# Order of side work in a two-layer decoder trunk: FFN sums leave PSUM behind the next split, modulation sums are planned away from the heads, two turned blocks are kept, the rope's swap moves to VectorE

## The chip, the cores and the metric

The kernel runs on one core of one Trainium2 chip. Its time is device microseconds of one execution; the version before was run three times, and the median stands for it. Five engines of the core take part: TensorE (PE in the profile; PEld are its weight loads), VectorE (DVE), ScalarE (ACT), GpSimd (POOL) and the queue of SyncE (SP), from which nearly all loads are issued.

## The reference, cut to what matters

One sequence of 256 tokens with 2048 features passes two layers. Layer 0 mixes by causal pooling, layer 1 by latent attention with 16 heads; each is followed by a SwiGLU feed-forward net (FFN) of width 5632. Every part reads `modulate(rmsnorm(x))`, with shift and scale out of a vector `c`, and adds its output times a gate that comes from `c` as well:

```python
shift_m, scale_m, gate_m, shift_f, scale_f, gate_f = jnp.split(sc @ mod_w[i] + mod_b[i], N_MOD, axis=-1)
ckv = rmsnorm(h_kv @ w_dkv, kv_norm)          # 512 wide, shared by all heads
k_nope, v = ckv @ w_uk, ckv @ w_uv            # per head 128 and 128
k_rope = apply_rope(h_kv @ w_kr, cos, sin)    # 64 wide, one for all heads
cq = rmsnorm(h @ w_dq, q_norm)
q = cq @ w_uq                                 # per head 128 + 64, rope on the 64
o = softmax(causal(q k)) v;  y = o @ w_o
x = x + gate_m * y;  x = x + gate_f * (silu(h @ w_gate) * (h @ w_up)) @ w_down
```

All is float32.

## The kernel before, in words

**Products.** A weight matrix is loaded in units of 128 x 2048 elements (1 MB). `split` makes two halves of a unit for TensorE: ScalarE rounds it to the upper half (L374), VectorE subtracts that from the unit to get the lower half (L376). Activations are split alike, and a product is three products: upper x upper, upper x lower, lower x upper. A unit then takes 24 matmuls of 128 x 512 (L398), or, in the keys, 48 of 128 x 256 (L1288). The loads have six buffers (`raw`), the halves six (`hl`, so three units), PSUM has eight banks (`ps`), all handed round in the order of the program.

**Modulation sums.** The products of `c` with `mod_w` and `kv_mod_w` are mostly made by VectorE: `Part.unit` loads 1 MB and sums 128 rows of it against `c` (L210, L211). 168 such units lie in a list, `background`, and are worked off beside other work. `plan(left, units)` sets a rate: so many sums until `left` remain, spread evenly over the next `units` splits. `split` calls `tick`, which starts a sum when the rate says so; `hold` stops that for a while, `release` sets a new rate. The constants `FFN0_UNITS`, `MLA_LATE` and their like (L64, L69) are the numbers behind these calls. When the 16 sums of a gate are there, VectorE adds the bias (L300), TensorE turns the column (L292), and DMAs write it to DRAM and spread it over the 128 partitions (`gate_to`).

**Stages.** After a prologue (pooling mixer) and FFN 0 comes a handover: `then_attention` orders ScalarE, VectorE and TensorE by hand. The last product of FFN 0 (L407) is interleaved with the normalization of the finished token tile: POOL takes the root (L472), the tile is scaled by it (`scale`, L476: the first 512 features on VectorE, the second on POOL), turned by TensorE (L482), modulated on ScalarE and VectorE (L490 to L503), and multiplied with `w_dkv` (L407; for the third and fourth 512 features L1197). `key_part` (L1208) makes the rotary key. Then `keys_values` runs for four groups of four heads: a unit of `w_uk` (L1288), a unit of `w_uv` (L398). Between the second and third group the hidden blocks of the queries begin: `hidden_q` scales (L530), turns (L540) and modulates (L558 to L560) 512 features each. Four units of `w_dq` give the query latent, `Latent` normalizes and turns it beside the fourth group. Then come the heads, in pairs: `project_heads` (L1368 to L1370, L1288), `probabilities` (L1383 to L1401), `turned` (L1407), `output` (L1414), and last `w_o` and FFN 1.

**FFN.** `down` sums three chunks of the middle layer in PSUM and then moves them at once: for the first group of chunks ScalarE copies them to `x` (L782), later VectorE adds them (L784).

**Rope.** `rope_start` copies the product out of PSUM by ScalarE, once as it is (L843) and once with halves of 32 rows swapped (L845, four instructions); `rope_end` multiplies by `sin_t` and `cos_t` on VectorE (L849, L850) and adds (L852).

Outside the hand-ordered stages a scheduler orders each engine's instructions by priority when the program is built; on the chip each engine runs them in that order.

Of the kernel before, what the change touches and what calls it, by code (L numbers as in the profile page):

```python
# [17 lines left out]
P = 128  # L18
# [45 lines left out]
FFN0_UNITS, MLA_UNITS, HEAD_UNITS, WO_UNITS, FFN1_UNITS = 95, 4, 16, 8, 60  # L64
# [4 lines left out]
LATE, MLA_LATE, WO_LATE = 3, 5, 3  # L69
# [4 lines left out]
def shape_constants():  # L74
# [6 lines left out]
    con[:, C_SIGN] = np.where(q % ROPE < HALF, -1.0, 1.0)  # L81
# [12 lines left out]
def tile_trunk(ctx: ExitStack, tc: tile.TileContext, a: dict, out: bass.AP):  # L94
# [190 lines left out]
    def gate_to(name, first):  # L285
# [163 lines left out]
    class Handover:  # L449
# [24 lines left out]
        def scale(self, tok, j):  # L474
            self.turned[tok, j] = t2k([P, CH]), ps_t().rearrange("p (k t) -> p k t", k=KL), t2k([P, KL, P])
            (dve if j == 0 else pool).tensor_scalar(out=self.turned[tok, j][0], in0=x[:, tok, j * CH:(j + 1) * CH],  # L476
                                                    scalar1=self.rstd[:, tok:tok + 1], scalar2=None, op0=ALU.mult)
# [236 lines left out]
    def ffn(l, hT, gate_name, begun, then):  # L714
# [22 lines left out]

        def down(i):
# [101 lines left out]
    def rope_start(bank):  # L840

        t_ = t2k([P, 2, T])
        act.activation(t_[:, 0, :], bank, AF.Copy)  # L843
        for r in range(0, P, HALF):
            act.activation(t_[r:r + HALF, 1, :], bank[r ^ HALF:(r ^ HALF) + HALF], AF.Copy)  # L845
        return t_

    def rope_end(t_, dsts):
        dve.tensor_tensor(out=t_[:, 1, :], in0=t_[:, 1, :], in1=sin_t, op=ALU.mult)  # L849
        dve.tensor_tensor(out=t_[:, 0, :], in0=t_[:, 0, :], in1=cos_t, op=ALU.mult)  # L850
# [264 lines left out]
    plan(n_all + MLA_LATE, FFN0_UNITS)  # L1115

    hkv, rstd, ckv = None, None, []
# [4 lines left out]
    def then_attention(old, banks, piece):  # L1122
# [6 lines left out]
        split_upper(w[0])  # L1129
        run(h.old(0))  # L1130
# [6 lines left out]
        split_lower(w[0])  # L1137
# [28 lines left out]
        run(b0[2], a1[2], b1[0], b1[1])  # L1166
# [4 lines left out]
        pieces = [scaled(rstd, j, pool) for j in range(2, ND)]  # L1171
        for j in range(2, ND):
            w_ = w_load_of(dkv(j))
            if j == 2:
                wkr = raw_t([P, KD, ROPE])
                sync.dma_start(wkr, a["w_kr"].rearrange("(k p) n -> p k n", p=P))
# [3 lines left out]
            full = [t2k([P, 2, T]) for _ in range(2)]  # L1180
            columns = [[cols[:, i, j * KL + k:j * KL + k + 1] for i in (C_AKV, C_SKV)] for k in range(KL)]
# [3 lines left out]
            for k, (by, plus) in enumerate(columns):  # L1185
# [13 lines left out]
        wkr_h, wkr_l = hl_t([P, KD, 2, ROPE]), hl_t([P, KD, 2, ROPE])  # L1199
        for i in range(2):  # L1200
            act.activation(wkr_h[:, :, i, :], wkr, AF.Copy)
# [3 lines left out]
        def key_part(n):  # L1205
            w_, i = sums[n]
            for k in range(KD):
                pe.matmul(krb[:, :T], lhsT=w_[:, k].rearrange("p i n -> p (i n)"), rhs=hkv[k // KL][:, i, k % KL, :],  # L1208
# [6 lines left out]
        for ks in (slice(0, KD // 2), slice(KD // 2, KD)):  # L1215
            for i in range(2):
                dve.tensor_tensor(out=wkr_l[:, ks, i, :], in0=wkr[:, ks], in1=wkr_h[:, ks, i, :].bitcast(F32),
                                  op=ALU.subtract)
# [72 lines left out]
    release(n_all, MLA_UNITS)  # L1291
# [13 lines left out]
    def last_of_background():  # L1305
        plan(n_all, 0)
# [9 lines left out]
    rope_end(kr_t, [(slice(0, ROPE), krT[0:ROPE, 0, :]), (slice(ROPE, P), krT[ROPE:P, 1, :])])  # L1316
# [261 lines left out]
```

## Time and profile before

| what | value |
|---|---|
| three runs | 1917.03, 1918.83, 1919.51 us; median 1918.83 |
| profiled execution | 1918.19 us, of which the span 1916.4 us |
| TensorE busy | 1862.8 us of the span |
| VectorE, ScalarE, POOL busy | 1402.7, 850.2, 26.9 us |
| mean granted TensorE clock | 0.987 |
| DMA | 574.98 MB, mean 300 GB/s |

The span runs from the first to the last instruction of the program. The profile gives starts and durations of every instruction, what an engine waited for, and by stretches of time the busy share and the granted clock. In it, FFN 0 reaches to about 889 us, the handover and the latent to 938, keys and query latent to 1010, the heads to 1098, `w_o` to 1186, FFN 1 to the end.

### The profile page before, as it was taken

What the parts mean: (1) busy time and instruction counts of PE and PEld (TensorE: products, weight loads), DVE (VectorE), ACT (ScalarE), POOL (GpSimd) and SP (SyncE); (2) the same over time, 40 slices, a digit from 0 to 9 for tenths busy, and PEclk for the clock granted to TensorE, in tenths of its full rate; (3) what the DMA queues carried; (4) which work ended last, traced back from release to release, by engine and by line L of the source; (5) the groups of instructions that cost most, each with busy time, mean ns of one, the idle gap of its engine ahead of it and who ended that gap; (6) DMA issues with size and microseconds to landing.
All of it is one profiled execution on the core that took longest, in us unless ns stands there. A gap on an engine that the chain in (4) does not pass through costs nothing.

```text
span 1916.4 us, 21930 instructions
## 1 busy us (share of the span) xinstructions
PE 1862.8 (97%) x8813; PEld 1507.8 (79%) x8813; DVE 1402.7 (73%) x1391; ACT 850.2 (44%) x958; POOL 26.9 (1%) x32
## 2 busy tenths in 40 slices
PE   7689999999999999999999999999999999999998
PEld 3255888888888888887889888888888888888887
DVE  2148799999788777799899966889785556645556
ACT  3125643444433334244678745634444433343343
POOL 0000000000000000002100000000000000000000
PEclk9789999999999999999999999999999999999999
DMA  9999998879998888897597775988776666665651
GB/s 399 398 418 417 368 364 333 319 299 361 357 344 332 327 330 326 332 373 274 212 371 291 293 278 194 397 318 335 260 284 240 241 240 239 249 222 205 220 198 44
DMA packets 86647, 574.98 MB, mean 300 GB/s; under 512 B 10977, under 2 KB 15505, under 8 KB 18321
## 3 DMA queue, kind: packets, MB, share of 16 engines
q1 hardware_dynamic: 86018, 570.42, 77.8%
q0 software_dynamic: 432, 3.15, 0.4%
q8 instruction: 69, 1.13, 0.2%
q14 instruction: 32, 0.26, 0.0%
q10 hardware_dynamic: 96, 0.02, 0.0%
HBM read 567.24 MB, written 6.32 MB: 299 GB/s over the span
## 4 chain that ended last, share of the span: by engine, by line
PE 69%; issue 22%; DMA 3%; DVE 3%; ACT 1%; SPq 0%; POOL 0%; POOLq 0%; DVEq 0%; ACTq 0%
PE ps L398 58%; DMA raw<-in_mod_w_dram 3%; PE ps L256 2%; PE ps L973 2%; PE ps L407 2%; PE ps L1288 2%; DVE raw L211 1%; PE ps L729 1%; PE ps L1197 1%; PE ps L540 0%; DMA raw<-in_mod_block_dram 0%; PE ps L196 0%; PE ps L948 0%; PE ps L770 0%; DVE hl L376 0%
## 5 line engine op out<-in xcount | busy, mean ns | idle before, releaser
L398 PE MATMUL ps<-hl,act 128*128 128x512 f32 x6744 | 1539.5, 390 | 1.9 <-DVE hl L376 1.0
L398 PEld LDWEIGHTS ps<-hl,act 128*128 128x128 f32 x6744 | 1263.0, 188 | 264.7 <-DVE hl L376 1.8
L376 DVE TENSOR_TENSOR hl<-raw,hl 128x2048 fp32r<-128x2048 f32 x289 | 661.1, 2289 | 253.2 <-ACT hl L374 252.5
L374 ACT ACTIVATE hl<-raw 128x2048 fp32r<-128x2048 f32 x289 | 553.1, 1918 | 647.8 <-PE ps L398 572.1
L211 DVE SCALAR_TENSOR_TENSOR raw<-raw,s_row 128x2048 f32<-128x2048 f32 x168 | 383.2, 2284 | 3.6 <-DMA raw<-in_mod_wt_dram 3.6
L256 PE MATMUL ps<-raw,s_strip 128*32 128x512 f32 x392 | 65.2, 760 | 34.6 <-DMA raw<-in_mod_w_dram 33.5
L698 DVE TENSOR_TENSOR act<-ps,act 128x512 f32<-128x512 f32 x96 | 64.5, 685 | 17.5 <-PE ps L398 17.5
L256 PEld LDWEIGHTS ps<-raw,s_strip 128*32 128x32 f32 x392 | 9.5, 121 | 70.0 <-DMA raw<-in_mod_w_dram 46.3
L784 DVE TENSOR_TENSOR x<-ps,x 128x512 f32<-128x512 f32 x32 | 22.1, 690 | 38.8 <-PE ps L398 38.8
L1288 PE MATMUL ps<-act,hl 128*128 128x256 f32 x384 | 49.6, 287 | 0.0
L1288 PEld LDWEIGHTS ps<-act,hl 128*128 128x128 f32 x384 | 48.3, 195 | 0.7 <-DVE act L1253 0.2
L407 PE MATMUL ps<-hl,act 128*128 128x512 f32 x192 | 47.0, 400 | 1.2 <-DVE act L503 1.2
L732 ACT ACTIVATE act<-ps 128x512 fp32r<-128x512 f32 x44 | 23.6, 594 | 50.0 <-PE ps L729 37.6
L407 PEld LDWEIGHTS ps<-hl,act 128*128 128x128 f32 x192 | 35.2, 188 | 10.7 <-ACT act L490 2.3
L263 DVE COPY t2k<-ps 128x256 f32<-128x256 f32 x4 | 1.7, 425 | 52.9 <-ACT t2k L262 52.9
L427 ACT ACTIVATE junk<-x 128x512 bf16<-128x512 f32 x23 | 14.5, 629 | 53.2 <-DVE x L612 37.6
L802 DVE TENSOR_TENSOR t2k<-ps,t2k 128x512 f32<-128x512 f32 x24 | 16.5, 689 | 28.5 <-PE ps L398 28.5
L798 ACT ACTIVATE t2k<-ps 128x512 f32<-128x512 f32 x24 | 14.2, 590 | 47.9 <-PE ps L398 47.9
L973 PEld LDWEIGHTS ps<-act,act 128*128 128x128 f32 x128 | 24.7, 200 | 11.6 <-issue 8.4
L696 ACT ACTIVATE act<-ps 128x512 f32<-128x512 f32 x32 | 19.1, 597 | 29.0 <-PE ps L398 28.8
L973 PE MATMUL ps<-act,act 128*128 128x256 f32 x128 | 31.9, 402 | 0.0
L733 DVE TENSOR_TENSOR act<-ps,act 128x512 fp32r<-128x512 f32 x44 | 28.1, 683 | 0.9 <-ACT act L732 0.9
(222 smaller groups left out, 911.6 us busy)
## 6 DMA issues: line engine op xcount, KB each, us to landing
raw<-in_mod_wt_dram SPq DMA_DIRECT2D x136, 1024.0 KB, 5.8
raw<-in_ffn_gate_dram SPq DMA_DIRECT2D x88, 1024.0 KB, 5.8
raw<-in_ffn_up_dram SPq DMA_DIRECT2D x88, 1024.0 KB, 5.1
raw<-in_ffn_down_dram SPq DMA_DIRECT2D x88, 1024.0 KB, 5.2
raw<-in_mod_w_dram SPq DMA_DIRECT2D x48, 1024.0 KB, 12.1
raw<-in_kv_mod_wt_dram SPq DMA_DIRECT2D x32, 1024.0 KB, 7.1
raw<-in_w_o_dram SPq DMA_DIRECT2D x16, 1024.0 KB, 6.1
raw<-in_mod_block_dram SPq DMA_DIRECT2D x8, 1024.0 KB, 12.5
```

The costliest lines, as they stand in the source:

```text
L211: dve.scalar_tensor_tensor(out=r, in0=r, scalar=1.0, in1=s_row, op0=ALU.mult, op1=ALU.mult, accum_out=self.sums[:, self.n:self.n + 1])
L256: pe.matmul(self.bank[m * STRIP:(m + 1) * STRIP, :], lhsT=weights(k), rhs=r[:, k, i, :], start=first, stop=last)
L374: hi_ins = act.activation(hi, r, AF.Copy)
L376: lo_ins = dve.tensor_tensor(out=lo, in0=r, in1=hi.bitcast(F32), op=ALU.subtract)
L398: pe.matmul(banks[tok], lhsT=t_[:, i, k, tok * P:(tok + 1) * P], rhs=w[:, k, :], start=first and n < len(part), stop=last and n >= len(ord ...
L407: pe.matmul(bank, lhsT=t_[:, i, k, tok * P:(tok + 1) * P], rhs=w[:, k, :], start=first and n == 0, stop=last and n == len(order) - 1)
L698: dve.tensor_tensor(out=part, in0=banks[tok], in1=part, op=ALU.add)
L732: act.activation(m[:, 0, :, ts_], v, AF.Copy)
L733: dve.tensor_tensor(out=m[:, 1, :, ts_], in0=v, in1=m[:, 0, :, ts_].bitcast(F32), op=ALU.subtract)
L784: dve.tensor_tensor(out=x[:, tok, js], in0=banks[tok], in1=x[:, tok, js], op=ALU.add)
L973: pe.matmul(mixed[g][:, n % 2, :], lhsT=wp[g][:, k, ns], rhs=pool_all[g // 2][:, g % 2, k, :], start=k == 0, stop=k == KL - 1)
L1288: pe.matmul(pt[:, h, :], lhsT=w(h0 + h, k), rhs=t_[:, i, k, :], start=n == 0, stop=n == 3 * KL - 1)
```

## The change

1. **FFN sums.** `down` no longer moves its sums at once: it hangs the move into `pending`, and the next split issues it behind its own two halves. A gate's `spread` waits for one split more.
2. **Where the modulation sums go.** FFN 0 leaves 62 of them instead of 69; the keys take 8 until 54 are left (before: 5, until 64), the four `w_dq` units take 6 until 48, and nothing is planned for the heads (before: 19 over `w_dq` and heads). `hold` comes one block of features earlier at the end of an FFN.
3. **Handover.** Both `scale`s run on VectorE; the lower half of the first `w_dkv` unit is made earlier; one pair of products swaps places.
4. **Kept blocks.** The turned third and fourth block of the latent are copied out of PSUM by ScalarE (four copies of 128 x 512) and kept; for the queries, `hidden_q` modulates these copies and neither scales nor turns the two blocks again. (Shift and scale are the queries' own.)
5. **Rope.** ScalarE's five copies go; VectorE multiplies straight out of PSUM, twice over 64 rows by `sin_t` with the halves swapped, once over 128 rows by `cos_t`. `w_uq` and `w_kr` are laid out on the host for that, so their loads have long rows (`w_kr` is 1 MB instead of 0.5), and `w_uq` goes through `split` as one piece of 128 x 1536.

```diff
-FFN0_UNITS, MLA_UNITS, HEAD_UNITS, WO_UNITS, FFN1_UNITS = 95, 4, 16, 8, 60
+FFN0_UNITS, MLA_UNITS, DQ_UNITS, WO_UNITS, FFN1_UNITS = 93, 4, 5, 8, 60
-LATE, MLA_LATE, WO_LATE = 3, 5, 3
+LATE, MIX_LATE, MIX_DQ = 3, 14, 6
...
-            pending.append((0, spread))
+            pending.append((1, spread))
...
-            (dve if j == 0 else pool).tensor_scalar(out=self.turned[tok, j][0], in0=x[:, tok, j * CH:(j + 1) * CH],
-                                                    scalar1=self.rstd[:, tok:tok + 1], scalar2=None, op0=ALU.mult)
+            dve.tensor_scalar(out=self.turned[tok, j][0], in0=x[:, tok, j * CH:(j + 1) * CH],
+                              scalar1=self.rstd[:, tok:tok + 1], scalar2=None, op0=ALU.mult)
...
-                if last and j == ND - 1:
+                if last and j == ND - 2:
                     hold()
...
-                    elif i == 0:
-                        act.activation(x[:, tok, js], banks[tok], AF.Copy)
                     else:
-                        dve.tensor_tensor(out=x[:, tok, js], in0=banks[tok], in1=x[:, tok, js], op=ALU.add)
+                        pending.append((0, lambda bank=banks[tok], sums=x[:, tok, js]: gather(bank, sums, i == 0)))
...
-        act.activation(t_[:, 0, :], bank, AF.Copy)
-        for r in range(0, P, HALF):
-            act.activation(t_[r:r + HALF, 1, :], bank[r ^ HALF:(r ^ HALF) + HALF], AF.Copy)
+        for r in range(0, P, ROPE):
+            other = slice(r ^ ROPE, (r ^ ROPE) + ROPE)
+            dve.tensor_tensor(out=t_[r:r + ROPE, 1, :], in0=bank[other], in1=sin_t[other], op=ALU.mult)
+        dve.tensor_tensor(out=t_[:, 0, :], in0=bank, in1=cos_t, op=ALU.mult)
...
-    plan(n_all + MLA_LATE, FFN0_UNITS)
+    n_all -= n_mix
+    plan(n_all + MIX_LATE, FFN0_UNITS)
...
-        run(b0[2], a1[2], b1[0], b1[1])
+        run(a1[2], b0[2], b1[0], b1[1])
...
+            for pt, dst in zip(pts, kept[-1]):
+                act.activation(dst, pt, AF.Copy)
...
-    release(n_all, MLA_UNITS)
+    release(n_all + MIX_DQ, MLA_UNITS)
...
-        pts = turned_pieces(pieces)
-        if len(hmx) < ND - 1:
+        pts = turned_pieces(pieces) if len(hmx) < 2 else kept[len(hmx) - 2]
+        if len(hmx) < 1:
             pieces = scaled(rstd, len(hmx) + 1)
...
-        plan(n_all, 0)
+        plan(n_all + MIX_DQ, 0)
...
-    plan(n_all - n_mix - WO_LATE, HEAD_UNITS)
+    plan(n_all, DQ_UNITS)
...
-    release(n_all - n_mix - WO_LATE, HEAD_UNITS - 8)
+    release(n_all, 1)
```

The order of the instructions changes with it. Three places matter below. First ScalarE in the keys, before: L374 makes upper halves (`raw_6485` is the third group's unit of `w_uv`, `raw_6586` the first of `w_dq`), L1280 and L1289 empty PSUM banks, L558 and L559 modulate the queries' first block.

```order
L374 ACTIVATE hl_6487<-raw_6485 128x2048
L1280 ACTIVATE act_6283<-ps_6349 128x512
L374 ACTIVATE hl_6592<-raw_6586 128x2048
L1289 ACTIVATE act_6385<-ps_6400 128x512
L1289 ACTIVATE act_6385<-ps_6426 128x512
L558 ACTIVATE t2k_6467<-ps_6452,cols 128x256
L558 ACTIVATE t2k_6471<-ps_6452,cols 128x256
L559 ACTIVATE act_6466<-t2k_6467 128x256
```

The same place of the changed kernel (L1297 is before's L1289, `raw_6516` the third unit of `w_uv`, `raw_6599` the first of `w_dq`):

```order
L1297 ACTIVATE act_6415<-ps_6457 128x512
L558 ACTIVATE t2k_6498<-ps_6483,cols 128x256
L558 ACTIVATE t2k_6502<-ps_6483,cols 128x256
L559 ACTIVATE act_6497<-t2k_6498 128x256
L559 ACTIVATE act_6497<-t2k_6502 128x256
L558 ACTIVATE t2k_6506<-ps_6488,cols 128x256
L558 ACTIVATE t2k_6510<-ps_6488,cols 128x256
L559 ACTIVATE act_6497<-t2k_6506 128x256
L559 ACTIVATE act_6497<-t2k_6510 128x256
L374 ACTIVATE hl_6518<-raw_6516 128x2048
L374 ACTIVATE hl_6604<-raw_6599 128x2048
```

The upper half of the third `w_uv` unit stood ahead of the block's eight instructions and stands behind them now. TensorE's own order is the same in both there: the third `w_uk` unit, the block's eight transposes, the third `w_uv` unit.

Second, VectorE at the same place, before: the lower halves (L376) of the third `w_uk` and `w_uv` unit, and sums (L211) between them.

```order
L376 TENSOR_TENSOR hl_6397<-raw_6386,hl_6396 128x2048
L211 SCALAR_TENSOR_TENSOR raw_6352,sums_5279<-raw_6352,s_row 128x2048
L211 SCALAR_TENSOR_TENSOR raw_6388,sums_5279<-raw_6388,s_row 128x2048
L211 SCALAR_TENSOR_TENSOR raw_6391,sums_5279<-raw_6391,s_row 128x2048
L376 TENSOR_TENSOR hl_6488<-raw_6485,hl_6487 128x2048
```

And in the changed kernel (L856 is the rope's last addition for the key):

```order
L376 TENSOR_TENSOR hl_6428<-raw_6416,hl_6427 128x2048
L211 SCALAR_TENSOR_TENSOR raw_6382,sums_5661<-raw_6382,s_row 128x2048
L211 SCALAR_TENSOR_TENSOR raw_6418,sums_5661<-raw_6418,s_row 128x2048
L211 SCALAR_TENSOR_TENSOR raw_6421,sums_5661<-raw_6421,s_row 128x2048
L211 SCALAR_TENSOR_TENSOR raw_6424,sums_5661<-raw_6424,s_row 128x2048
L560 TENSOR_TENSOR act_6497<-t2k_6498,act_6497 128x256
L560 TENSOR_TENSOR act_6497<-t2k_6502,act_6497 128x256
L560 TENSOR_TENSOR act_6497<-t2k_6506,act_6497 128x256
L560 TENSOR_TENSOR act_6497<-t2k_6510,act_6497 128x256
L856 TENSOR_TENSOR krT<-t2k_6208 32x256
L376 TENSOR_TENSOR hl_6519<-raw_6516,hl_6518 128x2048
```

One sum more, the block's four lower halves and a piece of the key's rope moved ahead of that split.

Third, TensorE at the start of the heads in the changed kernel: the last values (L398), the turning of the attention gate's column (L292), then the first pair's rope product (L1367 to L1369 are before's L1368 to L1370).

```order
L398 MATMUL ps_6848<-hl_6855,act_6199 128x512 x8
L398 MATMUL ps_6848<-hl_6856,act_6199 128x512 x4
L292 MATMUL ps_6894<-con,cols 16x128
L1367 MATMUL ps_6901<-act_6838,hl_6891 128x256
L1368 MATMUL ps_6901<-act_6838,hl_6890 128x256
```

VectorE writes that column in L300; in the changed kernel it stands there:

```order
L211 SCALAR_TENSOR_TENSOR raw_6851,sums_5661<-raw_6851,s_row 128x2048
L1261 SCALAR_TENSOR_TENSOR act_6838<-ps_6828,vcol,act_6838 128x256 x2
L376 TENSOR_TENSOR hl_6891<-raw_6888,hl_6890 128x1536
L1261 SCALAR_TENSOR_TENSOR act_6838<-ps_6833,vcol,act_6838 128x256 x2
L376 TENSOR_TENSOR hl_6947<-raw_6944,hl_6946 128x1536
L300 TENSOR_TENSOR cols<-sums_5661,vcol 128x16
```

Before, L292 and L300 of this gate stood in the last third of the heads; they moved to their start, with L300 behind the lower halves of the first two pairs' weights.

Counted over VectorE's whole order, the 168 sums lie so: before, 98 up to the handover's first L470, 13 from there to the query latent's last half, 15 to the first gated sum of `w_o`, 2 to the last one, 40 after it; in the changed kernel 105, 15, 6, 2 and 40.

More of the change, by code (lines that the diff above doesn't have):

```diff
@@ L80, in shape_constants @@
     con[:, C_FREQ] = freq[q % HALF]
-    con[:, C_SIGN] = np.where(q % ROPE < HALF, -1.0, 1.0)
+    con[:, C_SIGN] = np.where(q < ROPE, 1.0, -1.0)
     for i in range(NSTRIP):
@@ L736, in ffn, with gather @@
         stream_end = []
+        def gather(bank, sums, first):
+            if first:
+                act.activation(sums, bank, AF.Copy)
+            else:
+                dve.tensor_tensor(out=sums, in0=bank, in1=sums, op=ALU.add)
         def down(i):
@@ L1129, in then_attention @@
         split_upper(w[0])
+        split_lower(w[0])
         run(h.old(0))
@@ L1171, in then_attention @@
         pieces = [scaled(rstd, j, pool) for j in range(2, ND)]
+        mem = act_t([P, 2, KL, T], F32)
+        both = [mem[:, i] for i in range(2)]
         for j in range(2, ND):
@@ L1180, in then_attention @@
             full = [t2k([P, 2, T]) for _ in range(2)]
+            kept.append([both[j - 2][:, 2 * h2:2 * h2 + 2] for h2 in range(2)])
             columns = [[cols[:, i, j * KL + k:j * KL + k + 1] for i in (C_AKV, C_SKV)] for k in range(KL)]
@@ L1336, in tile_trunk @@
     HG = 2
-    w_uq = a["w_uq"][0]
+    w_uq = a["w_uq"]
     class Heads:
@@ L1544, in columns @@
         return np.asarray(v).reshape(-1, P).T
-    o = {n: np.asarray(i[n]) for n in ("x", "c", "positions", "mod_w", "pool_w", "w_kr", "w_uq", "final_norm")}
+    o = {n: np.asarray(i[n]) for n in ("x", "c", "positions", "mod_w", "pool_w", "final_norm")}
     o["vectors"] = np.concatenate([columns(i[n]) for n in (
```

45 lines of the change are left out of this document (19 added, 26 removed).

## The prediction

> **What bounds the kernel now.** I read the page first, then busy time by stages, then the timeline at each place where TensorE pauses. From the page, the span, the engines' shares, the granted clock and three groups:
>
> ```profile
> span 1916.4 us, 21930 instructions
> PE 1862.8 (97%) x8813; PEld 1507.8 (79%) x8813; DVE 1402.7 (73%) x1391; ACT 850.2 (44%) x958; POOL 26.9 (1%) x32
> PEclk9789999999999999999999999999999999999999
> L376 DVE TENSOR_TENSOR hl<-raw,hl 128x2048 fp32r<-128x2048 f32 x289 | 661.1, 2289 | 253.2 <-ACT hl L374 252.5
> L374 ACT ACTIVATE hl<-raw 128x2048 fp32r<-128x2048 f32 x289 | 553.1, 1918 | 647.8 <-PE ps L398 572.1
> L211 DVE SCALAR_TENSOR_TENSOR raw<-raw,s_row 128x2048 f32<-128x2048 f32 x168 | 383.2, 2284 | 3.6 <-DMA raw<-in_mod_wt_dram 3.6
> ```
>
> TensorE is the bound: every product goes through it, and the number of products hardly changes. So only three things can move the time: matmuls that go, pauses of TensorE, its clock. Stages, with PE, PEld, DVE, ACT and POOL busy, then clock, DMA share and GB/s:
>
> ```profile
> 476.00:900.00 424.00, 422.84 (x1898) 350.20 (x1896) 339.55 (x270) 163.99 (x121) 1.33 (x3) 1.00 0.88 338
> 900.00:938.00 38.00, 35.17 (x189) 28.40 (x190) 27.11 (x39) 27.90 (x53) 15.76 (x9) 1.00 0.34 118
> 938.00:1011.00 73.00, 72.96 (x433) 64.24 (x433) 69.71 (x77) 54.45 (x87) 3.01 (x2) 1.00 0.94 361
> 1011.00:1098.00 87.00, 84.59 (x574) 78.22 (x573) 83.76 (x173) 70.31 (x185) 0.61 (x1) 0.98 0.78 287
> 1186.00:1420.00 234.00, 234.00 (x1057) 194.25 (x1056) 198.92 (x178) 112.21 (x103) 0.00 (x0) 1.00 0.86 325
> ```
>
> TensorE is idle for 1.16 us up to 900 (FFN 0 and the handover's first wait), 2.83 in the rest of the handover and the latent, 0.04 in the keys, 2.41 in the heads, nothing in FFN 1. VectorE is busy for 96% of the keys (69.71 of 73) and of the heads: there a sum more or less can show; in the FFNs (80 and 85%) not.
>
> The profiled execution took 1918.19 us, its span 1916.4 and 1.8 around it; the median of the runs is 0.64 above, which I add at the end.
>
> **Kept blocks.** The chain of waits has the turning of one block for the queries:
>
> ```profile
> 966.98 0.87 PE ps L540 x8
> ```
>
> Two blocks are no longer turned: 2 x 0.87 = -1.74, on the bound itself. The four copies that replace them are like L1280 below (0.61 each); ScalarE, busy for 27.90 of 38 us there, makes them beside the `w_dkv` products: 0, or 0.6 if the second block's modulation had to wait for one.
>
> **Handover.** Its timeline, with what released each wait:
>
> ```profile
> 894.28 2.29 DVE L211 SCALAR_TENSOR_TENSOR raw<-raw,s_row 128x2048 f32<-128x2048 f32 x1
> 899.87 0.49 DVE L476 TENSOR_SCALAR t2k<-x,rstd 128x512 f32<-128x512 f32 x1 [0.69 <-POOL rstd L472]
> 899.93 3.98 POOL L476 TENSOR_SCALAR t2k<-x,rstd 128x512 f32<-128x512 f32 x1
> 900.41 0.66 PE L482 MATMUL ps<-con,t2k 128*128 128x128 f32 x4 [1.41 <-DVE t2k L476]
> 903.97 0.66 PE L482 MATMUL ps<-con,t2k 128*128 128x128 f32 x4 [0.80 <-POOL t2k L476]
> 912.88 4.37 PE L407 MATMUL ps<-hl,act 128*128 128x512 f32 x18 [1.18 <-DVE act L503]
> ```
>
> The waits are 1.41, 0.80 and 1.18; all idle time of the two rows of stages is 1.16 + 2.83 = 3.99, so -4.0 is the most to be had. The 0.80 goes: VectorE's 0.49 takes the place of POOL's 3.98. No sum stands before the last tile any more, which takes some of the 1.41, but the root on POOL (L472) stays in that chain; of the 1.18 the swapped products cover up to 0.8. What is late next is L503, which now stands behind both scales on VectorE. I take half, -2.0, bounds -4.0 and +1.0 (two more scales of 0.49 ahead of each L503).
>
> The Trainium skill ("GPSIMD Engine Reference", 4.1 Engine selection) calls GpSimd roughly line-rate where there is one input. The rows of 3.98 beside VectorE and 0.49 on VectorE differ from that, and the measurement decides; by the page the 0.80 could hardly exist, and the term would be -1.2.
>
> **Heads.** One wait in them, the clock right behind it, and the instructions that leave ScalarE:
>
> ```profile
> 1028.35 0.49 PE L1407 MATMUL ps<-con,t2k 128*128 128x128 f32 x3
> 1030.81 0.55 PE L1407 MATMUL ps<-con,t2k 128*128 128x128 f32 x3 [1.97 <-ACT t2k L1400]
> ```
>
> ```profile
> 1031.71:1035.12 3.41, 3.41 (x18) 3.41 (x18) 3.41 (x9) 2.74 (x9) 0.00 (x0) 0.50 0.79 312
> ```
>
> ```profile
> L845 ACT ACTIVATE t2k<-ps 32x256 f32<-32x256 f32 x36 | 13.5, 375 | 0.5
> L843 ACT ACTIVATE t2k<-ps 128x256 f32<-128x256 f32 x9 | 3.4, 375 | 3.8 <-PE ps L1370 2.1 <-ACT t2k L1409 0.9 <-PE ps L1208 0.8
> ```
>
> The wait at 1030.81 is followed by 3.41 us at half clock, which cost 1.7; with the 2.41 idle the heads lose 4.1. Per pair, ScalarE loses five copies of 0.375 (1.9), VectorE gets one instruction of about 0.42 more. Nine of 15 sums leave the heads, 9 x 2.2 = 20 us of VectorE's 83.76. So the probabilities, which come through both engines, are in time: -3.6, leaving 0.5 for small waits between pairs; bounds -4.1 and 0 (if the wait at 1030.81 has another cause than load).
>
> **Keys: a new wait.** This is the largest term. The order (in the section before) puts the upper half of the third `w_uv` unit behind the eight instructions that modulate the queries' first block. The same instructions before, where L374 behind them was only the unit after:
>
> ```profile
> 966.82 1.03 PE L540 MATMUL ps<-con,t2k 128*128 128x128 f32 x8
> 967.51 1.02 ACT L558 ACTIVATE t2k<-ps,cols 128x256 f32<-128x256 f32 x2
> 967.61 5.74 PE L398 MATMUL ps<-hl,act 128*128 128x512 f32 x24
> 969.92 0.74 ACT L559 ACTIVATE act<-t2k 128x256 fp32r<-128x256 f32 x2
> 970.54 1.93 ACT L374 ACTIVATE hl<-raw 128x2048 fp32r<-128x2048 f32 x1
> 971.79 1.43 DVE L560 TENSOR_TENSOR act<-t2k,act 128x256 fp32r<-128x256 f32 x4
> ```
>
> The eight can't begin before the turning they read; the half behind them ends at 970.54 + 1.93 = 972.47. TensorE wanted it at 967.61: +4.9. It then has eight products with the upper half (8 x 5.74/24 = 1.9), while VectorE's lower half takes 2.29 from 972.47: +0.4. Together +5.3, bounds +4.8 and +5.8. Nothing stands behind on TensorE that could run instead. The wait is longer than the 1.97 that the clock answered before, so half clock may follow: +1.4, bounds 0 and +1.7; in the handover waits up to 1.41 were answered by none.
>
> The Trainium skill ("TensorE: Matmul & The Clock Gate", Part 1) says that the clock falls back after at least one idle window of about 3.4 us. The row of 0.50 behind a wait of 1.97 doesn't fit that, and stays the measure; the rule returns as a rival.
>
> Ahead of that, at the first groups' start, an upper half stands among the evictions of `w_dkv`: +0.4, bounds 0 and +1 (part of one 1.9 half).
>
> VectorE's whole work from the lower half of the third `w_uk` to that of the last `w_uv` unit is, by the order, eight halves (18.3), nine sums (20.6), 16 L560 in four groups of 1.43 (5.7) and about 2 for latent and key: 46.6 with their recorded overlaps counted double, some 1.2 less in truth. TensorE needs eight units of 5.74 and two turnings, 47.7, plus the wait above. So VectorE keeps up on the whole, but with no room between two wanted halves. For the last `w_dq` units +0.5, bounds 0 and +3 (one sum and a bit). The transfers can add to it:
>
> ```profile
> raw<-in_w_dq_dram SPq DMA_DIRECT2D x4, 1024.0 KB, 9.5
> ```
>
> The keys move 361 GB/s, and `w_kr` adds half a megabyte at their beginning (1.5 us at that rate): 0 while six buffers run ahead.
>
> **Heads' start: a second wait.** L292 stands ahead of the first pair and needs L300, which stands behind the second pair's lower half. Before:
>
> ```profile
> 1004.58 5.74 PE L398 MATMUL ps<-hl,act 128*128 128x512 f32 x24
> 1008.81 0.61 ACT L1280 ACTIVATE act<-ps 128x512 f32<-128x512 f32 x1
> 1010.16 0.28 PE L1368 MATMUL ps<-act,hl 128*128 128x256 f32 x1
> ```
>
> ```profile
> L1362 ACT ACTIVATE hl<-raw 128x1024 fp32r<-128x1024 f32 x8 | 8.4, 1052 | 0.0
> L1363 DVE TENSOR_TENSOR hl<-raw,hl 128x1024 fp32r<-128x1024 f32 x8 | 9.8, 1219 | 0.0
> ```
>
> Now ScalarE empties the first bank of values, then makes the second pair's upper half (128x1536: 1.5 x 1.05 = 1.6), VectorE the lower one (1.5 x 1.22 = 1.8), then L300 (about 0.2). The bank is full halfway through the unit (1004.58 + 2.87 = 1007.45), ScalarE came to it at 1008.81 before; the chain 0.6 + 1.6 + 1.8 + 0.2 = 4.2 then ends between 1011.6 and 1013.0, where TensorE wanted 1010.2. As ScalarE has less to do there now, I take a value near the early end minus the overlap of neighbouring records: +1.9, bounds +1.3 and +2.7. That is the size of the wait of 1.97: half of its 1.7 for the clock, +0.8.
>
> **What costs nothing.** FFN 0 takes seven more sums, 16 us over 400: VectorE goes from 80 to 84%, as in FFN 1, where TensorE isn't idle. The FFN sums behind the next split are two of 0.69 that nothing waits for before the bank comes round; without that cover (a bank wanted at once) +2 in all. FFN 1 has no idle time to win.
>
> **Sum.** -1.74 - 2.0 - 3.6 + 5.3 + 1.4 + 0.4 + 0.5 + 1.9 + 0.8 = +3.0: 1918.19 + 3.0 = 1921.2, as a median 1921.8. The measurement can tell about 0.2%, 3.84 us, from no change, so that is "same", near its upper edge (1922.67).
>
> **Rivals.** *VectorE falls behind in keys and `w_dq`* (0.33): its reserve there is about 1 us, so one load that lands later than the 9.5 above, or one sum more ahead of a wanted half than I walked, passes to TensorE in full; one to two sums of 2.2 give 1924.0 to 1926.2. For it: 96% busy, DMA share 0.94. Against: the new wait of 5.3 lets VectorE catch up. It decides where VectorE's work between two wanted halves exceeds a unit's 5.74 by more than the first of them stood ahead.
>
> *Everything saved, little lost* (0.20): -1.74 - 4.0 - 4.1, and the new waits at +4.8 and +1.3 without clock: -3.7, 1915.1; a shorter wait at the third `w_uv`, if ScalarE's chain overlaps more than its records show, takes it to 1914. For it: those waits are short enough that a few tenths less in a chain close them. Against: the order leaves the 4.8 no cover.
>
> *The clock falls only after long pauses* (0.05): then before's half clock was no answer to the 1.97, the heads win 1.9 only, and the wait at L292 costs no clock: 3.0 + 1.7 - 0.8 = +3.9, 1922.7, counted as slower. The Trainium skill's clock gate rule above would mean this.
>
> That the change doesn't empty the heads is half so: by the order six sums still stand there, which is in the term.
>
> **Numbers.** The forecast has 0.42, so faster 0.20, same 0.42, slower 0.38. By the terms' bounds the likeliest case alone reaches from 1917 to 1925; with the two large rivals 1914.5 to 1927.
>
> **What would show it.** Right: a wait of TensorE of about 5 us ahead of the third `w_uv` unit, released by ScalarE's L374, with half clock behind it; a wait at L292 released by VectorE's L300; none of POOL's at L482; none near 2 us at L1407; FFN windows as full as before. The forecast is wrong if the first wait is under 3 us or over 7, if waits for L376 stand in the four `w_dq` units, or if FFN 0's window loses more than 3 us.

## The result and the profile after

The changed kernel took 1928.20 us (median of five runs, 1926.41 to 1928.87), the kernel before 1918.76 beside it: a ratio of 1.0052, interval 1.0041 to 1.0063. The forecast was 1921.8 in a range of 1914.5 to 1927: the sign of the shift was right, the size was not, and the measured time lies outside the range.

The page after, the three rows that answer to those before:

```profile
span 1926.6 us, 21881 instructions
PE 1864.0 (97%) x8797; PEld 1506.4 (78%) x8797; DVE 1408.6 (73%) x1394; ACT 832.3 (43%) x904; POOL 20.9 (1%) x30
PEclk9789999999999999999999999999999999999999
```

The rows hide the change: shares and clock look alike. Sixteen matmuls are gone (8813 before), POOL has lost its two scales, ScalarE 18 us. What tells more is the start of the first product of each stage. The table holds differences of such starts on TensorE, in us:

| stage | before | after | difference |
|---|---|---|---|
| to FFN 0's first turning (L729) | 388.85 | 389.59 | +0.7 |
| rest of FFN 0, to the handover's first product (L407) | 499.94 | 505.11 | +5.2 |
| handover and latent, to the keys' first product | 49.17 | 48.49 | -0.7 |
| keys and query latent, to the first pair's first product | 72.21 | 78.51 | +6.3 |
| heads, to the last `output` | 87.57 | 86.18 | -1.4 |
| rest, to the last product | 810.08 | 810.09 | 0.0 |

The sum is +10.1, the difference of the spans (1926.6 - 1916.4 = 10.2). Of the whole loss, 5.2 lies where the forecast had zero. What TensorE waits for, from the changed kernel's waits by line (total, times, longest; rows of the prologue left out):

```profile
PE ps L398 <- ACT hl L374: 6.5, 5, 4.6
PE ps L398 <- DVE hl L376: 2.1, 4, 0.6
...
PE ps L292 <- DVE cols L300: 2.0, 1, 2.0
PE ps L482 <- DVE t2k L476: 1.8, 1, 1.8
PE ps L1407 <- ACT t2k L1400: 1.1, 1, 1.1
```

Two of these are the forecast waits, nearly at their forecast size. At the third `w_uv` unit:

```profile
971.89 1.04 PE L540 MATMUL ps<-con,t2k 128*128 128x128 f32 x8
972.59 1.01 ACT L558 ACTIVATE t2k<-ps,cols 128x256 f32<-128x256 f32 x2
...
975.61 3.72 ACT L374 ACTIVATE hl<-raw 128x2048 fp32r<-128x2048 f32 x2
977.58 7.36 PE L398 MATMUL ps<-hl,act 128*128 128x512 f32 x24 [4.65 <-ACT hl L374]
```

and at the heads' start:

```profile
1019.77 1.75 DVE L376 TENSOR_TENSOR hl<-raw,hl 128x1536 fp32r<-128x1536 f32 x1
1021.44 0.17 DVE L300 TENSOR_TENSOR cols<-sums,vcol 128x16 f32<-128x16 f32 x1
1021.66 0.28 PE L292 MATMUL ps<-con,cols 128*16 128x128 f32 x1 [1.96 <-DVE cols L300]
```

The first reader of the half unit comes 4.65 us late, behind eight instructions of ScalarE; L292 comes 1.96 late, right behind L300. Both are followed by half clock (windows of 4.5 us from the end of each wait; the clock is the third number from the right):

```profile
977.58:982.08 4.50, 4.50 (x13) 3.54 (x14) 4.41 (x5) 1.75 (x1) 0.00 (x0) 0.62 1.03 428
1021.66:1026.16 4.50, 4.50 (x26) 4.50 (x27) 3.45 (x5) 0.31 (x2) 0.00 (x0) 0.62 0.94 323
```

0.62 over 4.5 us is 1.7 us lost in each. FFN 0 was not forecast. Four waits in it look like this one:

```profile
632.70 0.60 ACT L802 ACTIVATE t2k<-ps 128x512 f32<-128x512 f32 x1 [14.17 <-PE ps L398]
633.19 1.91 ACT L374 ACTIVATE hl<-raw 128x2048 fp32r<-128x2048 f32 x1
...
635.15 1.21 PE L398 MATMUL ps<-hl,act 128*128 128x512 f32 x4 [0.45 <-ACT hl L374]
```

ScalarE had been idle for 14.17 us, waiting in L802 (the silu of a finished bank), and only then made the upper half that TensorE wanted. At the same place of the kernel before, the upper halves of the next two units (621.21 and 626.65) are made ahead of the two silus (L798), and TensorE doesn't wait:

```profile
621.21 1.92 ACT L374 ACTIVATE hl<-raw 128x2048 fp32r<-128x2048 f32 x1 [3.52 <-PE ps L398]
626.65 1.92 ACT L374 ACTIVATE hl<-raw 128x2048 fp32r<-128x2048 f32 x1 [3.52 <-PE ps L398]
631.18 0.60 ACT L798 ACTIVATE t2k<-ps 128x512 f32<-128x512 f32 x1 [2.62 <-PE ps L398]
633.90 0.60 ACT L798 ACTIVATE t2k<-ps 128x512 f32<-128x512 f32 x1 [2.12 <-PE ps L398]
```

The load was not the reason; this is its issue on SP's queue, the first of the chunk's `up` units:

```profile
615.90 0.33 SPq L387 DMA_DIRECT2D raw<-in_ffn_up_dram  x1
```

With a median of 7.0 us to landing in that stretch, it had been in place for some ten. In the order of the program before, at least one unit's upper half stands ahead of every silu of FFN 0; in the changed kernel four pairs of silus have none ahead, and those are the four waits, at 634, 679, 724 and 835 us. Two more waits, of 0.56 each, stand at the end of FFN 0 (875 and 891 us), for VectorE's L376. The recorded idle time of the six, 2.9 us, is less than the 5.2 lost: around the wait above two matmuls start 0.84 us apart where 0.23 is usual, and the next come after 0.34 and 0.24, so that the wait costs more than its 0.45.

### The profile page after: what moved, and what is told of

It is laid out like the page before. It is cut to its first block, busy times and chain, and to the rows that moved or that the text cites. A ratio compares the mean times of both kernels' runs of the same rounds, so it can differ in the third digit from the quotient of the medians.

```text
span 1926.6 us, 21881 instructions
## 1 busy us (share of the span) xinstructions
PE 1864.0 (97%) x8797; PEld 1506.4 (78%) x8797; DVE 1408.6 (73%) x1394; ACT 832.3 (43%) x904; POOL 20.9 (1%) x30
## 4 chain that ended last, share of the span: by engine, by line
PE 89%; DMA 4%; DVE 4%; issue 1%; ACT 1%; SPq 0%; POOL 0%; POOLq 0%; DVEq 0%; ACTq 0%
PE ps L398 76%; DMA raw<-in_mod_w_dram 3%; PE ps L1296 2%; PE ps L256 2%; PE ps L977 2%; PE ps L407 2%; DVE hl L376 1%; DVE raw L211 1%; PE ps L729 1%; ACT hl L374 1%; PE ps L1208 1%; DMA raw<-in_mod_block_dram 0%; PE ps L196 0%; DMA raw<-in_ffn_gate_dram 0%; PE ps L952 0%
## 5 line engine op out<-in xcount | busy, mean ns | idle before, releaser
L398 PE MATMUL ps<-hl,act 128*128 128x512 f32 x6744 | 1543.5, 390 | 9.5 <-ACT hl L374 6.5
L398 PEld LDWEIGHTS ps<-hl,act 128*128 128x128 f32 x6744 | 1263.6, 188 | 276.2 <-ACT hl L374 8.4
L376 DVE TENSOR_TENSOR hl<-raw,hl 128x2048 fp32r<-128x2048 f32 (+1 forms) x297 | 674.7, 2274 | 265.4 <-ACT hl L374 264.8
L374 ACT ACTIVATE hl<-raw 128x2048 fp32r<-128x2048 f32 (+1 forms) x297 | 564.1, 1906 | 614.4 <-PE ps L398 461.2
L211 DVE SCALAR_TENSOR_TENSOR raw<-raw,s_row 128x2048 f32<-128x2048 f32 x168 | 383.1, 2285 | 3.2 <-DMA raw<-in_mod_wt_dram 3.1
L407 PE MATMUL ps<-hl,act 128*128 128x512 f32 x192 | 47.0, 398 | 1.1 <-DVE hl L520 0.9
L802 ACT ACTIVATE t2k<-ps 128x512 f32<-128x512 f32 x24 | 14.1, 589 | 72.5 <-PE ps L398 72.5
L407 PEld LDWEIGHTS ps<-hl,act 128*128 128x128 f32 x192 | 35.2, 188 | 10.6 <-ACT act L490 1.5
L806 DVE TENSOR_TENSOR t2k<-ps,t2k 128x512 f32<-128x512 f32 x24 | 16.6, 690 | 28.7 <-PE ps L398 28.7
```

Of the source, the lines that this page charges most:

```text
L211: dve.scalar_tensor_tensor(out=r, in0=r, scalar=1.0, in1=s_row, op0=ALU.mult, op1=ALU.mult, accum_out=self.sums[:, self.n:self.n + 1])
L374: hi_ins = act.activation(hi, r, AF.Copy)
L376: lo_ins = dve.tensor_tensor(out=lo, in0=r, in1=hi.bitcast(F32), op=ALU.subtract)
L398: pe.matmul(banks[tok], lhsT=t_[:, i, k, tok * P:(tok + 1) * P], rhs=w[:, k, :], start=first and n < len(part), stop=last and n >= len(ord ...
L407: pe.matmul(bank, lhsT=t_[:, i, k, tok * P:(tok + 1) * P], rhs=w[:, k, :], start=first and n == 0, stop=last and n == len(order) - 1)
```

## The experiments

Theory: the new plan of the modulation sums costs the time, by moving halves behind other work on ScalarE's and VectorE's queues; the remaining edits gain a little. Rivals: the FFN sums that leave PSUM later, the handover edits, or VectorE's load itself.

**The parts.** `m_only` is the kernel before with edit 2 alone:

```diff
-FFN0_UNITS, MLA_UNITS, HEAD_UNITS, WO_UNITS, FFN1_UNITS = 95, 4, 16, 8, 60
+FFN0_UNITS, MLA_UNITS, DQ_UNITS, WO_UNITS, FFN1_UNITS = 93, 4, 5, 8, 60
...
+    plan(n_all + MIX_LATE, FFN0_UNITS)
```

> Kernel before with the new plan of the sums alone (constants, goals, hold). Theory 'the plan costs it': the plan makes ScalarE's order around the splits worse, so the small waits of FFN 0 (+3.5 us), the wait at the third w_uv unit (4.6 us and the slow clock behind it, +6.4) and the one at L292 (about 2 us) are all here: 1926 to 1930, FFN 0 waits of 0.45 us behind L798 as in the changed kernel. Rival 'sums leaving PSUM late' (edit 1 holds banks or ScalarE in FFN 0): no new waits in FFN 0, 1923 to 1926.

Measured: 1933.67, ratio 1.0075 (1.0061 to 1.0089), slower than the whole change. Its waits by line:

```profile
PE ps L398 <- ACT hl L374: 6.3, 5, 4.5
PE ps L1408 <- ACT t2k L1401: 3.5, 3, 2.5
PE ps L292 <- DVE cols L300: 1.8, 1, 1.8
```

All three places are there, the FFN 0 waits at the same steps, and a wait of 2.5 in the heads besides. So the plan alone makes the new waits in FFN 0, at the third `w_uv` unit and at L292; the one of 1.75 in the handover is not among them.

`all_but_plan` is the changed kernel with the old plan:

```diff
-    plan(n_all + MIX_LATE, FFN0_UNITS)
+    plan(n_all + MLA_LATE, FFN0_UNITS)
...
-    plan(n_all, DQ_UNITS)
+    plan(n_all - n_mix - WO_LATE, HEAD_UNITS)
```

> Changed kernel with the old plan of the sums. Theory 'the plan costs it': no new wait in FFN 0, none at the third w_uv unit; handover +1.0, kept blocks -1.7, heads -1 to -3.6 as ScalarE is free of the rope: 1914 to 1917.5. Rival 'the other edits cost it': FFN 0 still loses 3 us or more, 1919 to 1923.

Measured: 1917.32, ratio 0.9993 (0.9984 to 1.0001). No wait at a silu or at the third `w_uv` unit; FFN 0 499.96, as before; keys to heads 69.99 (before 72.21); heads 85.17 (87.57); but the handover 51.69 (49.17), a loss of 2.5 where +1.0 was expected. The next run shows the same without the rest. `handover_only`:

```diff
+        split_lower(w[0])
         run(h.old(0))
...
-        split_lower(w[0])
...
-        run(b0[2], a1[2], b1[0], b1[1])
+        run(a1[2], b0[2], b1[0], b1[1])
```

> Kernel before with the three handover edits alone. Theory 'the last tile's chain is root, scale and turning on one path, VectorE's queue ahead of it doesn't matter': TensorE idles 2.5 to 3.9 us in 890 to 938, about as before (2.83 + what lies ahead of 900): 1918 to 1920. Rival, the prediction's step: 2 us less, 1916 to 1917.

Measured: 1920.74, ratio 1.0009 (1.0000 to 1.0018); handover 51.79. Neither fits: it is worse than the theory's bound. The timeline of `all_but_plan` has the reason:

```profile
895.63 2.29 DVE L211 SCALAR_TENSOR_TENSOR raw<-raw,s_row 128x2048 f32<-128x2048 f32 x1
...
897.84 2.29 DVE L520 TENSOR_TENSOR hl<-raw,hl 128x2048 fp32r<-128x2048 f32 x1
900.04 0.15 DVE L465 TENSOR_REDUCE sm<-ssq 128x2 f32<-128x6 f32 x1
...
903.42 0.88 DVE L476 TENSOR_SCALAR t2k<-x,rstd 128x512 f32<-128x512 f32 x2 [0.69 <-POOL rstd L472]
...
903.96 1.11 PE L482 MATMUL ps<-con,t2k 128*128 128x128 f32 x4 [3.63 <-DVE t2k L476]
```

A sum and the moved lower half (L520), 4.4 us together, stand on VectorE ahead of the last tile's chain. The stage's waits of 0.3 us and more add up to 4.2 us, hardly more than before's 3.4; but behind this one the clock was 0.50 for the 4.5 us that follow, which costs up to 2.2, and none of before's waits there was followed by that. With the new plan the sum isn't there, and L520 alone makes the wait of 1.75.

`rope_and_kept` has edits 4 and 5 alone:

```diff
-        act.activation(t_[:, 0, :], bank, AF.Copy)
+            dve.tensor_tensor(out=t_[r:r + ROPE, 1, :], in0=bank[other], in1=sin_t[other], op=ALU.mult)
...
+            for pt, dst in zip(pts, kept[-1]):
+                act.activation(dst, pt, AF.Copy)
```

> Kernel before with the rope on VectorE, its weight layouts and the kept blocks, nothing else. Theory: kept blocks -1.74 in the w_dq units, heads -1 to -3.6 since 1.9 us of ScalarE per pair go: 1913.5 to 1916.5. Rival 'VectorE is the one that is late in the heads': heads unchanged or worse with 15 sums in them, 1917 to 1919.

Measured: 1920.95, ratio 1.0008 (0.9999 to 1.0017). Keys to heads 70.00, 2.2 less; heads 91.48, 3.9 more. Both miss: the loss is one wait, with a clock of 0.59 in the 4.5 us behind it:

```profile
1067.86 0.38 PE L292 MATMUL ps<-con,cols 128*16 128x128 f32 x1 [4.96 <-DVE cols L300]
```

Since `w_uq` goes through `split` now, the pending turning of the gate is issued in the middle of the heads, ahead of the sum that completes its column. VectorE is late there, as the rival has it, but for one instruction; in `all_but_plan`, where `spread` waits for one split more, L292 has no wait.

**The places, one by one.** `lower_back` is the changed kernel with that half where it was:

```diff
-        split_lower(w[0])
         run(h.old(0))
...
         h.scale(0, 1)
+        split_lower(w[0])
```

> Changed kernel with the lower half of the first w_dkv unit back behind the scales, as before; both scales on VectorE and the swap stay. Theory 'that half of 2.2 us now stands on VectorE in the last tile's chain': the wait at the first turning (1.75) falls under 0.5 and the handover gives back 1.3 to 2.6 us: 1925.5 to 1927. Rival 'the scales on VectorE cost it': the handover waits 3.5 us or more as now, 1927.5 to 1929.

Measured: 1926.62, ratio 1.0044 (1.0031 to 1.0056); handover 46.73, 1.8 less, and no wait over 0.9 in it. As expected: the half on VectorE's queue cost it, not the scales. `old_plan_lower_back` puts that and the old plan together (both diffs above).

> Changed kernel with the old plan and with that lower half back. All theories that stand so far added up: before, less kept blocks 1.7, less 2.4 in the heads, less 0.8 to 2 in the handover, FFN 0 as before: 1912.5 to 1914.5. Rival 'the old sum order needs POOL's scale to fill VectorE': handover as before or worse, 1915 to 1917.5.

Measured: 1914.09, ratio 0.9976 (0.9967 to 0.9985). Faster than both kernels.

`silu_behind` lets the silus of the changed kernel wait for the next split:

```diff
-                act.activation(sg, gb[tok], AF.Silu)
+                pending.append((0, lambda sg=sg, bank=gb[tok]: act.activation(sg, bank, AF.Silu)))
```

> Changed kernel with the silus of FFN 0 and 1 queued behind the next split's halves, as edit 1 does for the sums. Theory 'ScalarE waits in L802 with the next unit already loaded, only the order of its queue keeps L374 back': the four waits of 0.45 at 634, 679, 724 and 835 us go, 2.4 us less: 1925 to 1926.5. Rival 'the next unit's load is late, for want of buffers': the four waits stay, released by the DMA, 1928.

Measured: 1924.94, ratio 1.0037 (1.0025 to 1.0050); FFN 0 501.99, 3.1 less. The four waits are gone, with nothing else changed in what is loaded or summed: they came from the order of ScalarE's queue alone. Two waits of 0.56 and 0.52 at the end of FFN 0, for VectorE's L376, stay.

`uv_first` puts the third `w_uv` unit's halves ahead of the queries' first block:

```diff
+        halves[0] = hi_ins, lo_ins
...
         if between:
-            between()
+            w_early(a["w_uv"][:, g][0])
+            with tc.issue_after(halves[0][0].ins), tc.issue_after(halves[0][1].ins):
+                between()
```

> Changed kernel with the third w_uv unit's halves queued ahead of the queries' first block on ScalarE and VectorE. Theory 'only the place behind the eight instructions costs it': the wait of 4.65 and the slow clock go, 5 to 6.4 us less, 1922 to 1923.5. Rival 'the sums before it are in the way too': its load is issued at 964.8 behind sums, and VectorE makes four sums ahead of the lower half, so a wait of about 3 us for L376 takes the place: 1924.5 to 1927.

Measured: 1926.10, ratio 1.0038 (1.0024 to 1.0051). The trace is of a second run of the same kernel.

> The third w_uv unit's halves first, for a trace at full clock: two waits of about 1.5 us there, one for the upper half (its load is issued behind sums), one for the lower half (four sums ahead of it on VectorE), in place of one of 4.65; no half clock if each stays under 1.76. One wait of 3 or more for the lower half alone would say that the load is in time.

Measured: 1926.18. In its timeline L376 and L378 are the halves (L374 and L376 above), L401 the products:

```profile
965.14 0.33 SPq L390 DMA_DIRECT2D raw<-in_w_uv_dram  x1
973.61 1.91 ACT L376 ACTIVATE hl<-raw 128x2048 fp32r<-128x2048 f32 x1 [0.53 <-DMA raw<-in_w_uv_dram]
973.87 2.29 DVE L211 SCALAR_TENSOR_TENSOR raw<-raw,s_row 128x2048 f32<-128x2048 f32 x1
...
975.57 2.61 PE L401 MATMUL ps<-hl,act 128*128 128x512 f32 x8 [2.25 <-ACT hl L376]
...
977.82 2.29 DVE L378 TENSOR_TENSOR hl<-raw,hl 128x2048 fp32r<-128x2048 f32 x1
980.17 4.02 PE L401 MATMUL ps<-hl,act 128*128 128x512 f32 x9 [1.99 <-DVE hl L378]
```

The rival holds: the one wait becomes two, 2.25 for a load that took 8.4 us to land, and 1.99 for the lower half behind the fourth sum. So three things stand one behind another there: the place on ScalarE, the load, VectorE's sums. The unit itself got no cheaper: keys and query latent take 78.13 in place of 78.51, although the wait at L292 is gone as well, because the edit also brought L300 ahead of the first two pairs' lower halves (1017.80 us). Eight sums in the keys in place of five may be behind all three, as each takes a load, a buffer and 2.2 us; `heads_emptied` below, with five there, has no wait at this unit, but its order differs in more than that.

`gate_later` turns the attention gate's column four splits later:

```diff
-            pending.append((1, spread))
+            pending.append((5 if name == "mla" else 1, spread))
```

> Changed kernel with the turning of the attention gate's column four splits later. Theory 'L292 stands ahead of a sum that isn't ready': the wait of 1.96 us at the heads' start goes and the half clock of 3.4 us behind it, 3.4 to 3.7 us less in all: 1924.4 to 1925.2. Rival 'the first pair is late there anyhow': a wait for L1261 or L376 of about 1 us stays, no half clock, 1926 to 1926.5.

Measured: 1928.40, ratio 1.0050 (1.0038 to 1.0063). A miss for both: the wait at L292 is gone, and nothing is gained, because the heads wait later in its place:

```profile
1085.85 2.29 DVE L376 TENSOR_TENSOR hl<-raw,hl 128x2048 fp32r<-128x2048 f32 x1
1088.05 0.16 DVE L1399 RECIPROCAL sm<-sm 128x2 f32<-128x2 f32 x1
1088.24 0.40 ACT L1400 ACTIVATE t2k<-t2k,sm 128x128 f32<-128x128 f32 x1 [0.64 <-DVE sm L1399]
...
1088.70 1.08 PE L1407 MATMUL ps<-con,t2k 128*128 128x128 f32 x3 [2.57 <-ACT t2k L1400]
```

A `w_o` lower half stands ahead of the reciprocal; half clock follows as it did behind L292. It is not told apart whether the moved L292 alone put it there.

`mended` has all four repairs (the four diffs above).

> Changed kernel with four repairs together, the plan kept: lower half back (-1.6), silus behind the split (-3.1), third w_uv halves first (-2.1), gate's turning later (-3.5). If the places are independent: 1917.5 to 1919. Rival 'VectorE's sums just meet the next place': less than 7 us of the 10.3 come back, 1921 to 1924.

Measured: 1921.26, ratio 1.0013 (1.0003 to 1.0022): 6.9 of 10.3 come back, and the rival's range holds. Its reason isn't shown: the single repairs measured 1.6, 3.3, 2.1 and -0.2, together about 6.8, so what is missing from the 10.3 is the gate's 3.5, which `gate_later` alone didn't give. At the third `w_uv` unit `mended` waits 1.93 and 2.81, in the heads 2.26.

**Better versions.** `hold_earlier` is `old_plan_lower_back` with the changed kernel's earlier hold:

```diff
-FFN0_UNITS, MLA_UNITS, HEAD_UNITS, WO_UNITS, FFN1_UNITS = 95, 4, 16, 8, 60
+FFN0_UNITS, MLA_UNITS, HEAD_UNITS, WO_UNITS, FFN1_UNITS = 93, 4, 16, 8, 60
...
-                if last and j == ND - 1:
+                if last and j == ND - 2:
```

> The kernel with the old plan and the lower half back (1914.1), with the sums of FFN 0 held one block of features earlier and spread over 93 splits, so that 98 are still done there and ScalarE's order keeps a unit ahead. Theory 'a sum of 2.2 us ahead of the last tile makes the first wait of the handover': 1.41 falls under 0.4, 1912 to 1913.5. Rival 'the hold itself makes the two waits of 0.56 at the end of FFN 0': those come, 1.4 us, and use up the gain: 1914 to 1915.

Measured: 1912.58, ratio 0.9967 (0.9954 to 0.9979); handover 46.50, against 48.69 without the hold. The wait of 1.41 is gone; one of 0.55 for L806 has come near the end of FFN 0. This is the fastest version, 0.33% under the kernel before.

Three runs asked what emptying the heads is worth. `hold_and_silu` adds the silu diff to `hold_earlier`:

> The fastest kernel so far (old plan, lower half back, sums held earlier; 1912.6) with the silus queued behind the next split. Control: FFN 0 has no wait at the silus to lose there, so no change, 1911.5 to 1913.5. If the silus behind the split hold PSUM banks too long, FFN 1 loses: 1914 or more.

Measured: 1912.59, ratio 0.9968 (0.9955 to 0.9980); no change, as expected. `heads_emptied` does seven sums more in FFN 0:

```diff
-    plan(n_all + MLA_LATE, FFN0_UNITS)
+    plan(n_all - 7 + MLA_LATE, FFN0_UNITS)
...
-    release(n_all, MLA_UNITS)
+    release(n_all - 7, MLA_UNITS)
...
-        plan(n_all, 0)
+        plan(n_all - 7, 0)
```

> hold_and_silu with seven sums moved from the w_dq units and heads into FFN 0 (105 there, as in the changed kernel). Theory 'the heads gain from the rope leaving ScalarE, not from fewer sums, and FFN 0 only lost by its order': FFN 0 and heads as in the control, within 1 us of it. Rival, the prediction's step: heads lose 1 to 2 us less, 1910 to 1911.5. Rival 'FFN 0 is short of VectorE': 3 us or more slower than the control.

Measured: 1912.83, ratio 0.9974 (0.9964 to 0.9984). The heads take 83.95 in place of 85.22, the rival's gain of 1.3; FFN 0 501.95 in place of 500.69, a loss of 1.3 in two waits for L376, each behind a sum among the last moves; the second:

```profile
884.14 2.29 DVE L211 SCALAR_TENSOR_TENSOR raw<-raw,s_row 128x2048 f32<-128x2048 f32 x1
886.35 4.49 DVE L376 TENSOR_TENSOR hl<-raw,hl 128x2048 fp32r<-128x2048 f32 x2
```

`sums_earlier` spreads the same sums over 89 splits instead of 93:

> heads_emptied with the sums of FFN 0 spread over 89 splits in place of 93, so that none stands between the last block's moves. Theory 'the two waits at the end of FFN 0 come from sums between those moves': both go, 1.4 us less than heads_emptied (1912.8), heads stay at 84: 1911 to 1912. Rival 'FFN 0 is short of VectorE with 105 sums': the waits move to an earlier place, 1912.5 to 1914.

Measured: 1913.06, ratio 0.9977 (0.9968 to 0.9987). FFN 0 is 500.45 with 106 sums, so those waits belonged to the place of the last sums and not to their number; but the heads are 85.62 again, with a wait of 1.59. Counted in VectorE's order between the query latent's last half and the first gated sum of `w_o`, 13 sums stand in `hold_and_silu`, 12 in `heads_emptied`, 11 in `sums_earlier` and 6 in `uv_first`: the heads take 85.22, 83.95, 85.62 and (second run) 85.24. So their time doesn't follow the number; why one order is 1.3 better stays open. `kept_only` has edit 4 alone:

> Kernel before with the kept blocks alone. The prediction's count: 16 transposes less in the w_dq units, 1.74 us less from the first w_uk unit to the first pair, 1916.3 to 1917.5. Rival 'VectorE is the bound there': TensorE waits for halves instead, less than 0.7 us gained, 1918 to 1919.

Measured: 1918.05, ratio 1.0003 (0.9994 to 1.0011). Keys to heads 69.83, 2.4 less than before; heads 89.24, 1.7 more:

```profile
PE ps L1413 <- ACT t2k L1406: 2.6, 3, 2.0
PE ps L1420 <- ACT t2k L1415: 1.3, 1, 1.3
```

TensorE comes earlier to the heads and waits there for ScalarE (before, 2.2 and 0.2 for the same two). The gain exists and is given back where the next engine is late; in `all_but_plan`, with the rope off ScalarE, it stays.

## Why the prediction was wrong, by its steps

- **FFN 0 at nothing: the step that failed.** It argued that seven more sums are 4% of VectorE's time, and that no wait was there to gain. The share is about right (351 of 424 us, 83%); the waits came from the order of two queues, which the plan shifts when the program is built. Measured +5.2 (forecast 0, bound +2): 3.1 from ScalarE's queue, four pairs of silus without a half ahead (`silu_behind`; 0.78 a wait), and 2.1 in the two waits that it leaves, for VectorE's lower halves, where sums stand between the last moves. The step looked at the order in the keys and heads but not in FFN 0, where it tells the four waits. FFN 0 losing more than 3 us was one of the prediction's own signs of being wrong.
- **Handover -2.0.** Measured -0.7. "No sum stands before the last tile any more" was right, but the moved lower half, named in the change, takes its place on the same queue (1.75). With it back the stage gains 2.4 (46.73).
- **Heads -3.6.** Measured -1.4 with the 1.7 of half clock behind L292 inside, so -3.1 without it. Of the 3.6, 2.4 is there with the old plan (85.17); neither the handover edits (87.61) nor the kept blocks (89.24) give it alone, and `rope_and_kept` without its one wait (4.96) and the clock behind it (1.8) comes to 84.7, which points to the rope; no run has the rope alone. The sums that leave were given a share and have none that shows (6 to 13 sums, 85.2 to 85.6 in three of four orders). 83.95, the whole 3.6, came in one order only.
- **Third `w_uv` unit +5.3 and +1.4.** Right in place, releaser and clock: a wait of 4.65 and 1.7 in the clock. The wait is a little under the lower bound of 4.8, and the 0.4 for VectorE's lower half was not seen. The runs add that the order is only one of three things that stand there.
- **L292 +1.9 and +0.8.** The wait was right, 1.96. In the clock it cost 1.7; the 0.8 was half of that, as a chance, and a wait of this length does go either way (last section).
- **Kept blocks -1.74.** A little small: 2.4 less up to the heads with this edit alone. That the kernel keeps the gain was right only with the heads' ScalarE freed.
- **Start of keys +0.4, `w_dq` +0.5.** Nothing of either is seen.
- The rival "VectorE falls behind in keys and `w_dq`" didn't happen in the changed kernel, though `uv_first` shows how near it is. The rival that everything is saved gave 1915.1; the old plan with the lower half back measured 1914.09 and, with the earlier hold, 1912.58. The rival that the clock falls only after long pauses is refuted by the half clock behind the wait of 1.96.

So the failing step is the one that took a busy share for slack. The stages give +10.1 where the sum had +3.0: FFN 0 accounts for 5.2 of the 7.1, the handover for 1.3 and the heads with their clock for 1.4; the prologue adds 0.7 (its end lay between 387.7 and 390.8 us in the traces read here, whatever the kernel), and keys to heads took 1.5 less than its terms.

## What to carry to other kernels

Work that is "beside" the critical path costs by where it stands in each in-order queue, and a table that says how much of it to do where also decides what stands ahead of what on engines that it doesn't touch. Ahead of each instruction that waits for TensorE's result, look whether the next thing that TensorE needs is already made; in FFN 0 the count of such places in the old and the new order told the four waits to the piece. And price a saving at the end of the next stage, not where it is made: the kept blocks and the moved L292 both gave their gain back within 90 us.

## What the runs showed of the hardware

Whether half clock follows a wait depends on where the wait falls, not on its length alone. In each of the 17 traces read here, the granted clock changes only at times that lie whole steps of 3.413 us apart: in the changed kernel half clock begins at 977.80 and 1022.18, 13 steps apart. The steps lie differently against the program in each trace (before, half clock begins at 1031.71). Of all steps between 300 and 1880 us that begin at full clock, those in which TensorE's waits add up to 1.80 us or less are followed by a step at full clock, those with 1.82 or more by one at half clock. Here are a step and its successor in `m_only` (the wait of 1.82 lies in the first) and in `mended` (the wait of 2.26, of which 1.73 lies in the first and 0.53 in the second); PE busy is the second number:

```profile
1015.92:1019.33 3.41, 1.59 (x10) 1.16 (x8) 3.41 (x7) 3.41 (x7) 0.00 (x0) 1.00 0.87 248
1019.33:1022.74 3.41, 3.41 (x10) 2.63 (x9) 2.97 (x6) 1.33 (x4) 0.00 (x0) 0.50 0.95 312
```

```profile
1078.53:1081.94 3.41, 1.70 (x12) 1.31 (x10) 3.36 (x6) 2.87 (x8) 0.00 (x0) 1.00 0.67 271
1081.94:1085.35 3.41, 2.78 (x17) 2.35 (x18) 3.41 (x10) 2.79 (x9) 0.00 (x0) 1.00 0.68 221
```

So a wait of 1.82 to 2.57 us costs 1.7 us beyond its own time where 1.82 of it falls in one step, and nothing beyond where the next step divides it, as it did the 1.93 (0.78 and 1.15) and the 2.26 of `mended`. Behind the wait at the third `w_uv` unit TensorE ran at half clock for 3.4 us in the changed kernel and in `gate_later`, and for 4.8 and 5.3 in `lower_back` and `silu_behind`, whose wait was as long. A difference of up to 1.7 us between two traces can be this alone. The Trainium skill ("TensorE: Matmul & The Clock Gate", Part 1) has the clock fall back after at least one idle window of about 3.4 us; here 1.82 us of idle time in a step of 3.41 was enough, and the measurement decides.

A load of 1 MB took 5.1 to 5.8 us to land in the medians of the FFNs' and most sums' loads before. In the keys the third `w_uv` unit's took 8.4 (396 GB/s, DMA share 1.00 from 955 to 985 us in the second run of `uv_first`), no longer than the 9.5 of the `w_dq` loads before: it came late because it was issued late.
